# Adding the residual of a decoder block's second FFN layer: accumulating transfers in place of loads and GpSimd additions

## The chip, the cores and the metric

The kernel runs on one core of a Trainium2 chip. The metric is the device time of one execution in microseconds (us), the median of several runs. The engines are TensorE (PE in the profile, with PEld for its weight loads), VectorE (DVE), ScalarE (ACT), GpSimd (POOL) and SyncE (SP, which issues transfers). Each engine works through its own list of instructions in order; semaphores tie the lists together.

## What is computed

One block of a decoder: a token mixer with a residual, then an FFN with a residual, then a final norm. The change touches the FFN's second product and its residual.

```python
def reference(x, ...):
    ...
        h = h + jnp.einsum('bse,ed->bsd', mixed, w_out)
        hn2 = rmsnorm(h, norm2_g)
        up = jnp.einsum('bsd,df->bsf', hn2, w_up)
        act = jnp.square(jax.nn.relu(up))
        h = h + jnp.einsum('bsf,fd->bsd', act, w_down)
    return rmsnorm(h, final_g)
```

There are 2048 tokens, a model width of 1024 and an FFN width of 4096, all in float32.

## The kernel before

Tokens are split into four tiles of 512 (`T`), features into chunks of 128 (`P`), so that a chunk of one tile is 128 partitions x 512 columns. The residual `h` lies in DRAM as `hs[j]`, eight such chunks (256 KB each) for each token tile `j`.

Every matrix product is made of float32r parts: an operand is split into a high and a low part (`split`, L143: ACT copies the high part, DVE subtracts to get the low one), and three matmuls, high x high, high x low and low x high, make one product.

The FFN's second layer is the function `down` (L1068). It works on the tokens in two pairs of tiles, `PAIRS` = (0, 1) and (3, 2), called q = 0 and q = 1 below, and uses a fast scheme of seven block products, P1 to P7, in the order P1, P6, P7, P4, P5, P2, P3. P4 and P2 are split once more in the same manner and run for q = 1 and q = 0 together as 28 steps of 12 matmuls (`inner_step`, L1221, matmuls at L1230); the others run straight (matmuls at L1392) as eight steps. For each step, `make` or `make_inner` loads a weight block (tile `wr` or `wq`) and blocks of activations (`ar`), and splits them into `wd` and `ad` (L146 on ACT, L147 on DVE). Two or three steps are made ahead of their use; five buffers of `ad` and three of `wd` exist.

A product that is finished is taken out of PSUM by `evac` (L1199), for each q and each of four chunks n. After P1, ACT copies PSUM to the value tile `p1` (a sum that later becomes a half of the result). After P7, ACT copies to `u3` and `c21`. After P5, DVE adds PSUM to `u3` and to `u2` (L1201). The value tiles hold four chunks each. Into each chunk of `p1`, `c21`, `u3` and `u2` the residual is added once, by `add_residual` (L1194): 4 chunks x 4 tiles x 2 q = 32 additions, of which 8 follow P1, 8 follow P7 and 16 follow P5. The tile `res` that receives the residual has two buffers (the pool `rsp`, L1487).

Right after P5's last chunk, `final` (L1252) sums squares of the finished results of one token tile: ACT squares a chunk (`sq`, L1249) and DVE adds it to `ss` (L1250), first the four chunks of `c21`, then the four of `u3`. P2 comes after P5 on PE, and the splits of its operands stand between these squares and sums on ACT and DVE. P2 adds its inner products to `p1` on DVE (L1237), and P3 then adds to `u2`. A scheduler decides the order of instructions on each engine, from the order of the program and its own model of durations.

Of the kernel before, what the change touches and what calls it, by code (L numbers as in the profile page):

```python
# [8 lines left out]
F32 = mybir.dt.float32  # L9
# [4 lines left out]
ALU = mybir.AluOpType  # L14

P = 128
S = 2048
D = 1024
T = 512
# [21 lines left out]
DA = 2  # L41
# [5 lines left out]
def hymba_block(ctx: ExitStack, tc: tile.TileContext, xT, gains, w_in, pool_w, w_out, w_up, w_down, out):  # L47
    nc = tc.nc
# [84 lines left out]
    hs = [dram.tile([KD, P, T], F32, name=f"hs{j}") for j in range(NT)]  # L133
# [934 lines left out]
    def down(pools):  # L1068
        t8, s8, rs, rt, pupa, pup, rsp, rlp, tmp_, psb = pools
# [122 lines left out]
            return V[name, q]  # L1192

        def add_residual(t, j, half, n):  # L1194
            r = rsp.tile([P, T], F32, tag="res", name="res")
            nc.sync.dma_start(r, hs[j][4 * half + n])
            nc.gpsimd.tensor_tensor(t, t, r, ALU.add)

        def evac(n_, q, n):  # L1199
            b, (j0, j1) = ps[q, n], PAIRS[q]  # L1200
            add = lambda to, of: nc.vector.tensor_tensor(to[:, n], b, of[:, n], ALU.add)  # L1201
            if n_ in CHAIN:
                nc.scalar.activation(val(CHAIN[n_], q)[:, n], b, AF.Copy)
                if n_ == "P7":
                    nc.scalar.activation(val("c21", q)[:, n], b, AF.Copy)
                    add_residual(val("c21", q)[:, n], j1, 0, n)
                elif n_ == "P1":
                    add_residual(val("p1", q)[:, n], j0, 0, n)
            elif n_ == "P5":
                add(val("u3", q), val("u3", q))  # L1210
                add_residual(val("u3", q)[:, n], j1, 1, n)
                add(val("u2", q), val("u2", q))
                add_residual(val("u2", q)[:, n], j0, 1, n)
                if n == 3:
                    final(j1, [val("c21", q)[:, k] for k in range(4)] + [val("u3", q)[:, k] for k in range(4)])
            else:
                add(val("u2", q), val("u2", q))
                if q == 0 and n == 3:
                    final(j0, [val("p1", q)[:, k] for k in range(4)] + [val("u2", q)[:, k] for k in range(4)])
# [153 lines left out]
        for g, (n_, i, kk, qs_) in enumerate(steps):  # L1373
# [5 lines left out]
            t, left_ = made.pop(g)  # L1379
# [46 lines left out]
    def catch_up(n):  # L1426
        for _ in range(n):
            with ExitStack() as behind:
                for ins in (last_split[0], done[0]):
                    if ins:  # L1430
                        behind.enter_context(tc.issue_after(ins.ins))
                later.pop(0)()
# [42 lines left out]
    def ffn():  # L1475
        catch_up(len(later))
        front_scope.close()
        for _ in layer.pop():
            pass
        left_scope.close()  # L1480
        with ExitStack() as scope:
            spool = lambda name, bufs, **kw: scope.enter_context(tc.tile_pool(name=name, bufs=bufs, reuse_waits="tile", **kw))

            rlp, pupa = spool("rlp", 2), spool("pupa", 2)
            spool("even", 1).tile([P, 2 * P // 4], F32, name="even")
            rs, rt, t8 = spool("rs", 5), spool("rt", 6), spool("t8", DA + 1)
            s8, tmp2, pup, rsp = spool("s8", 2 * DA + 1), spool("tmp2", 2), spool("pup", 6), spool("rsp", 2)  # L1487
            down([t8, s8, rs, rt, pupa, pup, rsp, rlp, tmp2, spool("psb", 1, space=PS)])

    x0_scope = inner.enter_context(ExitStack())  # L1490
# [20 lines left out]
    tail(True)  # L1511
    run()
    ffn()


    count = P * H * (TB * NT - 2)
    got = nc.values_load(zeros[0:1, 0:1], min_val=0, max_val=count)
    with tc.If(got < count):
        wlist.clear(), raws.clear(), grans.clear(), gates.clear(), marks.clear()
        state["gran"], last_split[0], last_mm[0], done[:] = 0, None, None, (None, None)  # L1520
        open_pools(front_scope)
        open_big(left_scope)
        open_att(att_scope)
        for j in range(NT):
            far(j)
        att_scope.close()
        open_last(front_scope, last_scope)
        open_out(out_scope)
        tail(False)
        run()  # L1530
        ffn()
# [44 lines left out]
```

## Time and profile before

| | |
|---|---|
| median of 3 runs | 1933.88 us (1931.08 to 1934.98) |
| profiled execution | 1934.94 us, its span 1933.1 us |
| granted TensorE clock | 0.995 |
| down projection | from 1309 us to the end |
| P1's residual additions | 1396 to 1423 us |
| P7's residual additions | 1570 to 1591 us |
| P5's residual additions | 1733 to 1778 us |
| P2 on PE | 1741.6 to 1823 us |

The page gives the busy time of each engine, the busy share by slices of time, the transfers, the chain of work that ended last, and groups of like instructions with their mean duration and the idle time before them. In a group's row, `x16` is the count, the number after the bar the busy time in us, then the mean in ns, then the engine's idle time just before these instructions and what ended it. In a row of stretches the columns are the length, the busy time and count of PE, PEld, DVE, ACT and POOL (or of fewer, where only one line's instructions are taken), the granted clock, the DMA engines' busy share and the GB/s. In a timeline row they are the start, the time taken, the engine, the line and the instruction. A row of waits reads: who waited, for whom, us in total, times, longest.

### The profile page before, as it was taken

To read this page: it belongs to the slowest core of one execution; us is meant where nothing else is said; L and a number is where in the kernel's file an instruction comes from. 1 tells how busy PE (TensorE), PEld (TensorE's weight loads), DVE (VectorE), ACT (ScalarE), POOL (GpSimd) and SP (SyncE) were. 2 spreads that over 40 slices of the span, in tenths; PEclk is the share of its full clock that TensorE was granted. 3 is DMA by queue.
4 is the path that set the end of the run, shared out by engine and by line. 5 is a ranking of instruction groups with operands and counts; after the bars stand their busy time and mean duration, and the time that the engine had idled before them with its cause. 6 is when DMAs were issued, how large, how long until landed. Compare 5 with 4: busy or idle time off the path is not lost.

```text
span 1933.1 us, 26290 instructions
## 1 busy us (share of the span) xinstructions
PE 1902.3 (98%) x9043; PEld 1586.1 (82%) x9043; DVE 1384.3 (72%) x2026; ACT 991.0 (51%) x1580; POOL 205.8 (11%) x399
## 2 busy tenths in 40 slices
PE   9999999999999999999999999999999999999997
PEld 7888888887888888888888888887888888887887
DVE  6887799668876875767678767676554558649874
ACT  5565566455544455555566555553333255425643
POOL 0211123102111120000000000000010020004120
PEclk9999999999999999999999999999999999999999
DMA  6685786888796864567567566679798869958852
GB/s 225 205 270 180 230 278 207 265 311 268 252 359 252 305 203 167 205 242 232 204 234 245 199 221 224 227 271 387 263 334 287 289 234 334 327 195 267 311 206 90
DMA packets 197359, 483.44 MB, mean 250 GB/s; under 512 B 22496, under 2 KB 42976, under 8 KB 193120
## 3 DMA queue, kind: packets, MB, share of 16 engines
q1 hardware_dynamic: 197072, 481.40, 72.2%
q8 instruction: 73, 1.20, 0.3%
q14 instruction: 70, 0.57, 0.1%
q10 hardware_dynamic: 144, 0.26, 0.0%
HBM read 320.10 MB, written 161.48 MB: 249 GB/s over the span
## 4 chain that ended last, share of the span: by engine, by line
PE 88%; DVE 6%; DMA 4%; issue 1%; ACT 1%; POOL 0%; SPq 0%; DVEq 0%; ACTq 0%
PE pb L1392 21%; PE pY L1052 17%; PE pZ L1052 8%; PE pd L175 7%; PE pd L177 7%; PE pd L176 7%; PE pb L1230 6%; PE pX L1052 4%; PE po L672 2%; PE pta L661 1%; PE pr L228 1%; PE pz L614 1%; PE pz L615 1%; PE pm L202 1%; DMA raw<-in_w_in_dram 1%
## 5 line engine op out<-in xcount | busy, mean ns | idle before, releaser
L1392 PE MATMUL pb<-ad,wd 128*128 128x512 f32 x1872 | 429.6, 391 | 4.8 <-ACT ad L146 4.8
L1392 PEld LDWEIGHTS pb<-ad,wd 128*128 128x128 f32 x1872 | 352.4, 189 | 78.4 <-ACT ad L146 5.2
L1052 PE MATMUL pY<-sa,hw 128*128 128x512 f32 x1536 | 364.2, 389 | 1.8 <-ACT u L987 1.8
L1052 PEld LDWEIGHTS pY<-sa,hw 128*128 128x128 f32 x1536 | 288.2, 188 | 62.3 <-ACT u L987 2.7
L175 PE MATMUL pd<-h,hl 128*128 128x512 f32 x752 | 299.9, 399 | 1.4 <-DVE acc L811 0.7
L177 PE MATMUL pd<-h,hl 128*128 128x512 f32 x752 | 297.0, 395 | 0.0
L176 PE MATMUL pd<-h,hl 128*128 128x512 f32 x752 | 296.7, 395 | 0.0
L146 ACT ACTIVATE ad<-ar 128x1024 fp32r<-128x1024 f32 x136 | 142.4, 1052 | 108.1 <-PE pb L1392 66.8
L147 DVE TENSOR_TENSOR ad<-ar,ad 128x1024 fp32r<-128x1024 f32 x136 | 173.3, 1286 | 34.2 <-ACT ad L146 34.2
L1052 PE MATMUL pZ<-sa,hw 128*128 128x512 f32 x768 | 184.6, 389 | 0.0
L1052 PEld LDWEIGHTS pZ<-sa,hw 128*128 128x128 f32 x768 | 144.1, 188 | 29.9
L175 PEld LDWEIGHTS pd<-h,hl 128*128 128x128 f32 x752 | 142.2, 189 | 29.3 <-issue 1.1
L177 PEld LDWEIGHTS pd<-h,hl 128*128 128x128 f32 x752 | 141.8, 189 | 28.0
L176 PEld LDWEIGHTS pd<-h,hl 128*128 128x128 f32 x752 | 142.0, 189 | 27.0
L146 ACT ACTIVATE hl<-raw 128x512 fp32r<-128x512 f32 x168 | 103.9, 630 | 106.7 <-PE pd L177 67.1
L1230 PE MATMUL pb<-ad,wd 128*128 128x512 f32 x672 | 154.1, 390 | 3.8 <-DVE ad L147 3.8
L1230 PEld LDWEIGHTS pb<-ad,wd 128*128 128x128 f32 x672 | 125.6, 188 | 32.0 <-DVE ad L147 6.1
L147 DVE TENSOR_TENSOR hl<-raw,hl 128x512 fp32r<-128x512 f32 x168 | 114.4, 687 | 51.2 <-ACT hl L146 48.0
L146 ACT ACTIVATE wd<-wr 128x1024 fp32r<-128x1024 f32 x48 | 50.9, 1062 | 152.1 <-PE pb L1392 138.5
L147 DVE TENSOR_TENSOR hw<-rt,hw 128x512 fp32r<-128x512 f32 x128 | 87.6, 688 | 56.6 <-ACT hw L146 55.8
L147 DVE TENSOR_TENSOR wd<-wr,wd 128x1024 fp32r<-128x1024 f32 x48 | 58.6, 1222 | 60.2 <-ACT wd L146 60.0
L1052 PE MATMUL pX<-sa,hw 128*128 128x512 f32 x384 | 93.1, 389 | 0.0
(213 smaller groups left out, 2626.0 us busy)
## 6 DMA issues: line engine op xcount, KB each, us to landing
ar<-sd SPq DMA_DIRECT2D x104, 512.0 KB, 5.7
rb<-in_w_up_dram SPq DMA_DIRECT2D x32, 1024.0 KB, 6.0
wr<-in_w_down_dram SPq DMA_DIRECT2D x64, 512.0 KB, 5.5
sd<-a SPq DMA_DIRECT2D x112, 256.0 KB, 3.5
raw<-in_w_in_dram SPq DMA_DIRECT2D x50, 512.0 KB, 4.6
sd<-s SPq DMA_DIRECT2D x96, 256.0 KB, 3.5
raw<-in_w_out_dram SPq DMA_DIRECT2D x32, 512.0 KB, 6.0
ar<-sdi SPq DMA_DIRECT2D x32, 512.0 KB, 5.6
```

The lines of the kernel that those rows point to most:

```text
L146: nc.scalar.activation(hi, src, AF.Copy)
L147: return nc.vector.tensor_tensor(lo, src, hi.bitcast(F32), ALU.subtract)
L175: nc.tensor.matmul(ps, hl[:, 0, c], hi, start=(k == 0), stop=False)
L176: nc.tensor.matmul(ps, hl[:, 0, c], lo, start=False, stop=False)
L177: mm = nc.tensor.matmul(ps, hl[:, 1, c], hi, start=False, stop=(k == n - 1))
L202: marks["pm"] = nc.tensor.matmul(pm[:, c:c + 1], ss[:, c * P:(c + 1) * P], inv[n], start=(i == 0), stop=(i == len(parts) - 1))
L228: mm = nc.tensor.matmul(pr[:, b * P:(b + 1) * P], yr[:, x, b:b + 1].to_broadcast([P, P]), identr, start=(b == 0 and x == 0), stop=(b == TB ...
L614: nc.tensor.matmul(pz, qa[:, qsl], k, start=first, stop=False, skip_group_check=not (first and last))
L672: nc.tensor.matmul(po[:, p * 256 + to:p * 256 + to + hi - lo], vw[:, 2 * p + v], at[:, x, lo:hi], start=(p == 0 and n == 0 and x == 0), sk ...
L1052: nc.tensor.matmul(t, w[:, wx, c], a[:, ax, c % 2], start=first and c == 0 and x == 0, stop=last and c == G - 1 and x == 2, skip_group_che ...
L1230: nc.tensor.matmul(b, t[:, wx, 2 * (kk % 2) + c, i * P:(i + 1) * P], a[:, ax, c], start=p in ("P1", "P5", "P2") and kk == 0 and c == 0 and ...
L1392: nc.tensor.matmul(ps[q, n], t[:, wx, c, n * P:(n + 1) * P], left_[q][:, ax, c], start=(n_ in ("P1", "P5", "P3") and kk == 0 and c == 0 an ...
```

## The change

`add_residual` loads nothing into a tile of its own any more. GpSimd issues one transfer for each chunk that reads the residual from DRAM and adds it onto the value tile in SBUF (`accum_op=ALU.add`). The pool `rsp` with its two tiles goes. As before, each of the 32 chunks has its own instruction, on the same engine and behind the same DVE or ACT instruction.

```diff
         def add_residual(t, j, half, n):
-            r = rsp.tile([P, T], F32, tag="res", name="res")
-            nc.sync.dma_start(r, hs[j][4 * half + n])
-            nc.gpsimd.tensor_tensor(t, t, r, ALU.add)
+            nc.gpsimd.dma_start(t, hs[j][4 * half + n], accum_op=ALU.add)
...
-            s8, tmp2, pup, rsp = spool("s8", 2 * DA + 1), spool("tmp2", 2), spool("pup", 6), spool("rsp", 2)
+            s8, tmp2, pup, rsp = spool("s8", 2 * DA + 1), spool("tmp2", 2), spool("pup", 6), None
```

The lines behind `add_residual` move up by two: L1201 becomes L1199, L1249 and L1250 become L1247 and L1248. PE's list is the same in both. The lists of DVE, ACT and SP differ in a few places.

DVE at the end of P5, before: `u3` and `u2` are the value tiles, `pb` the PSUM bank, `ss` the sum of squares, and the two splits of `ad` and `wd` are for P2.

```order
L1201 TENSOR_TENSOR u2_14505<-pb_15773,u2_14505 128x512
L1250 TENSOR_TENSOR ss_16297<-ss_16297,sq_16308 128x512
L1201 TENSOR_TENSOR u3_15079<-pb_15780,u3_15079 128x512
L1201 TENSOR_TENSOR u2_14505<-pb_15780,u2_14505 128x512
L147 TENSOR_TENSOR ad_16236<-ar_16234,ad_16236 128x1024
L1201 TENSOR_TENSOR u3_15125<-pb_15787,u3_15125 128x512
L1201 TENSOR_TENSOR u2_14534<-pb_15787,u2_14534 128x512
L1201 TENSOR_TENSOR u3_15125<-pb_15794,u3_15125 128x512
L1201 TENSOR_TENSOR u2_14534<-pb_15794,u2_14534 128x512
L1250 TENSOR_TENSOR ss_16297<-ss_16297,sq_16311 128x512
L1201 TENSOR_TENSOR u3_15125<-pb_15801,u3_15125 128x512
```

The same place of the change:

```order
L1199 TENSOR_TENSOR u2_14486<-pb_15738,u2_14486 128x512
L1199 TENSOR_TENSOR u3_15060<-pb_15745,u3_15060 128x512
L1199 TENSOR_TENSOR u2_14486<-pb_15745,u2_14486 128x512
L147 TENSOR_TENSOR ad_16201<-ar_16199,ad_16201 128x1024
L1199 TENSOR_TENSOR u3_15098<-pb_15752,u3_15098 128x512
L1199 TENSOR_TENSOR u2_14515<-pb_15752,u2_14515 128x512
L1248 TENSOR_TENSOR ss_16246<-ss_16246,sq_16257 128x512
L1199 TENSOR_TENSOR u3_15098<-pb_15759,u3_15098 128x512
L1199 TENSOR_TENSOR u2_14515<-pb_15759,u2_14515 128x512
L1199 TENSOR_TENSOR u3_15098<-pb_15766,u3_15098 128x512
L1199 TENSOR_TENSOR u2_14515<-pb_15766,u2_14515 128x512
```

The first sum with a square of `u3` stands five instructions later (behind the next two additions, a split and two more), and the second one moves behind the last addition, to the place just ahead of the weight split for P2's fifth step.

ACT at the same time, before: the squares `sq` of `u3` among the splits for P2.

```order
L146 ACTIVATE ad_16231<-ar_16227 128x1024
L1249 ACTIVATE sq_16308<-u3_15079 128x512
L146 ACTIVATE ad_16236<-ar_16234 128x1024
L1249 ACTIVATE sq_16311<-u3_15079 128x512
L146 ACTIVATE wd_16403<-wq_16401 128x1024
L146 ACTIVATE ad_16408<-ar_16404 128x1024
L1249 ACTIVATE sq_16314<-u3_15079 128x512
```

And of the change:

```order
L146 ACTIVATE ad_16196<-ar_16192 128x1024
L146 ACTIVATE ad_16201<-ar_16199 128x1024
L1247 ACTIVATE sq_16257<-u3_15060 128x512
L1247 ACTIVATE sq_16260<-u3_15060 128x512
L146 ACTIVATE wd_16336<-wq_16334 128x1024
L146 ACTIVATE ad_16341<-ar_16337 128x1024
L1247 ACTIVATE sq_16263<-u3_15060 128x512
```

The first square has moved behind a split; the second is still the last instruction ahead of the weight split.

SP at the same time, as a difference (`res` are the residual loads, `ar` and `wq` the blocks for P2):

```order
 L1141 DMA ar<-sdi_0_3_428 128x1024
-L1196 DMA res<-hs_281 128x512
-L1196 DMA res<-hs_282 128x512
-L1196 DMA res<-hs_281 128x512
 L1141 DMA ar<-sdi_1_0_429 128x1024
-L1196 DMA res<-hs_282 128x512
-L1196 DMA res<-hs_281 128x512
-L1196 DMA res<-hs_283 128x512
-L1196 DMA res<-hs_284 128x512
 L1136 DMA wq<-wi_P_0_461 128x1024
 L1141 DMA ar<-sdi_1_1_430 128x1024
```

The residual loads between P2's loads are gone, and P2's loads keep their order. On POOL, the 32 transfers stand in the places of the 32 additions; each goes by one of eight semaphores, and waits for the transfer eight before it.

## The prediction

> **What bounds the kernel now.** I read the page's first part, then the busy time by stretches, then the waits.
>
> ```profile
> PE 1902.3 (98%) x9043; PEld 1586.1 (82%) x9043; DVE 1384.3 (72%) x2026; ACT 991.0 (51%) x1580; POOL 205.8 (11%) x399
> PE pb L1392 <- ACT ad L146: 4.8, 1, 4.8
> PE pb L1230 <- DVE ad L147: 3.8, 4, 1.3
> PE pY L1052 <- ACT u L987: 0.7, 1, 0.7
> ACT sq L1249 <- POOL u L1197: 8.7, 4, 3.4
> ```
>
> TensorE (PE) has work nearly throughout, so an edit on another engine counts only where it starves PE or feeds it sooner. The waits of the last 600 us leave two places of size: 4.8 us where the down projection begins (at 1310 us, before any residual is added), and 3.8 us in the matmuls of L1230, where PE waits for a split that VectorE (DVE) makes. L1230 runs twice, once as product P4 and once as product P2, with 336 equal matmuls each time. Busy time in these two stretches:
>
> ```profile
> 1578.56:1654.72 76.16, 76.16 (x336) 62.72 (x335) 1.00 0.86 302
> 1741.60:1823.18 81.58, 77.78 (x336) 62.34 (x335) 1.00 0.86 300
> ```
>
> P4 takes 76.16 us, P2 takes 81.58 (the columns are length, PE busy, weight loads busy, clock, DMA share, GB/s). The clock is 1.00 in both. So P2 loses **5.42 us**, a little more than the labelled 3.8. The timeline shows where:
>
> ```profile
> 1752.84 2.63 PEld L1230 LDWEIGHTS pb<-ad,wd 128*128 128x128 f32 x12 [0.17 <-DVE ad L147]
> 1759.05 6.06 PE L1230 MATMUL pb<-ad,wd 128*128 128x512 f32 x25 [0.57 <-DVE ad L147]
> 1766.46 5.51 PE L1230 MATMUL pb<-ad,wd 128*128 128x512 f32 x23 [1.35 <-DVE ad L147]
> 1772.67 5.74 PE L1230 MATMUL pb<-ad,wd 128*128 128x512 f32 x24 [0.71 <-DVE ad L147]
> 1779.59 43.59 PE L1230 MATMUL pb<-ad,wd 128*128 128x512 f32 x191 [1.17 <-DVE ad L147]
> ```
>
> The stalls lie between 1752 and 1779 us, and then 191 matmuls run without one. In the same time GpSimd (POOL) makes 16 of its 32 residual additions. DVE, all forms apart, from 1733 to 1778 (first four rows) and in a stretch without POOL additions (last two):
>
> ```profile
> 1733.00:1778.00 45.00, 42.38 (x183) 33.69 (x182) 45.00 (x44) 22.88 (x28) 27.86 (x16) 1.00 0.76 248
> L147 DVE TENSOR_TENSOR ad<-ar,ad 128x1024 fp32r<-128x1024 f32 x10 | 15.8, 1590 | 0.0
> L147 DVE TENSOR_TENSOR wd<-wq,wd 128x1024 fp32r<-128x1024 f32 x6 | 10.7, 1786 | 4.2 <-ACT wd L146 4.2
> L1250 DVE TENSOR_TENSOR ss<-ss,sq 128x512 f32<-128x512 f32 x8 | 9.6, 1198 | 0.0
> ...
> L147 DVE TENSOR_TENSOR ad<-ar,ad 128x1024 fp32r<-128x1024 f32 x14 | 17.0, 1222 | 1.1 <-ACT ad L146 1.1
> L1250 DVE TENSOR_TENSOR ss<-ss,sq 128x512 f32<-128x512 f32 x3 | 2.1, 689 | 0.1
> ```
>
> DVE is busy for 45.00 of 45 us, but its instructions are longer than elsewhere: a split takes 1590 or 1786 ns in place of 1222, a sum of squares 1198 in place of 689. That is 10 x 0.368 + 6 x 0.564 + 8 x 0.509 = 3.7 + 3.4 + 4.1 = **11.2 us** of DVE time lost while POOL adds. POOL's additions are what differs between the stretches, so I take them for the cause. The Trainium skill, "SBUF — State Buffer", section "Who interferes with whom", says the same of a DVE instruction with two SBUF inputs beside a GpSimd instruction that reads SBUF, and that DMAs do not meet the engines' ports; by that rule all of the 11.2 us would come back.
>
> **The change, part by part.** *The 16 additions of P5.*
>
> ```profile
> L1197 POOL TENSOR_TENSOR u<-u,res 128x512 f32<-128x512 f32 x16 | 27.9, 1752 | 158.6 <-DVE u L1201 144.8 <-DMA res<-hs 13.1 <-DVE ss L1250 0.6
> 1733.15 1.28 DVE L1201 TENSOR_TENSOR u<-pb,u 128x512 f32<-128x512 f32 x2
> 1734.35 1.94 DVE L147 TENSOR_TENSOR ad<-ar,ad 128x1024 fp32r<-128x1024 f32 x1
> 1749.23 1.32 DVE L147 TENSOR_TENSOR wd<-wq,wd 128x1024 fp32r<-128x1024 f32 x1
> 1750.47 2.31 DVE L147 TENSOR_TENSOR ad<-ar,ad 128x1024 fp32r<-128x1024 f32 x1
> ```
>
> They take 27.9 us of POOL and go. What this gives PE is not 11.2 us but at most the 5.42 it loses. P2 has 28 steps of 12 matmuls, 76.16 / 28 = 2.72 us each; the fifth is due at 1741.60 + 4 x 2.72 = 1752.5, and its left operand was ready at 1750.47 + 2.31 = 1752.8: late from here on. I lay the new DVE order out with undisturbed durations (split 1.22, addition of PSUM 0.68, sum 0.69): pair of additions from 1733.15, split to 1735.6, six additions to 1739.7, split to 1740.9, pair to 1742.2, sum to 1742.9, six additions to 1747.0, sum to 1747.7, weight split to 1748.9, left split to **1750.1**. That is 2.4 us ahead of its due time, and the next ones stay ahead (seventh step: 1754.4, due 1757.9; ninth: 1760.8, due 1763.4). So if nothing new is waited for, P2 runs at 76.16 us.
>
> *What is new: the accumulating transfers.* No POOL transfer and no accumulation is in this trace. Nearest rows: the loads that go, all transfers on the same DRAM tensor, and the squares on ScalarE (ACT) that wait.
>
> ```profile
> L1196 SPq DMA_DIRECT2D res<-hs x32: 319/319/999, 1309.7 to 1772.2; - x32
> DMA to landing us min/median/max: 2.6/3.7/7.6
> ...
> DMA to landing us min/median/max: 2.1/4.4/10.5
> ...
> 1736.36 1.06 ACT L146 ACTIVATE ad<-ar 128x1024 fp32r<-128x1024 f32 x1 [0.48 <-PE pb L1392]
> 1739.67 0.63 ACT L1249 ACTIVATE sq<-u 128x512 f32<-128x512 f32 x1 [2.24 <-POOL u L1197]
> 1741.80 1.07 ACT L146 ACTIVATE wd<-wq 128x1024 fp32r<-128x1024 f32 x1 [1.50 <-PE pb L1392]
> 1749.50 0.63 ACT L1249 ACTIVATE sq<-u 128x512 f32<-128x512 f32 x1 [3.36 <-POOL u L1197]
> ```
>
> Issue on POOL: at least the 0.32 us that SP needs, at most the 1.75 us that POOL spent on the addition. Landing: at least 2.6 us, the fastest plain load; at most twice the slowest transfer on this tensor, 21 us, since source and destination both have to be read. I take 1 + 5 = **6 us** from the end of DVE's addition to landed data, nearer to the median load (3.7) than to twice the extreme. The price in a sentence of its own: the Trainium skill, "DMA: Bandwidth & Descriptors", section "Anatomy of one DMA — SWDGE (gpsimd) path", fits 2.0 us plus bytes over 436 GB/s, which for 256 KB is an estimate of 2.6 us, and would make the margin below wider.
>
> What waits for them: on ACT the squares of u3, and behind these the splits of P2; on DVE the sums. The first u3 tile is added by 1733.8, and DVE wants its square at 1742.2; less 0.63 for the square, that allows 7.7 us, and 10.1 with the 2.4 us that DVE is ahead. The second is added at 1736.3 and stands before the weight split of the fifth step on ACT, which must be done by 1747.7: 1747.7 - 1.06 - 0.63 - 1736.3 = 9.7 us, or 12.1. The fourth (added 1739.0) has 14.8 us by the seventh step's due time. With 6 us none of them holds anything. They are also quicker in sequence than before: there only two load buffers existed, so 16 additions ended at 1777 us (the 1749.50 row shows the fourth square waiting 3.36 us for POOL); now eight may be in flight.
>
> *The other 16 transfers.* P1's and P7's lie where PE has no idle time:
>
> ```profile
> 1396.00:1423.00 27.00, 27.00 (x121) 22.36 (x120) 18.12 (x13) 11.21 (x15) 11.43 (x8) 1.00 0.81 284
> 1570.00:1591.00 21.00, 21.00 (x94) 17.40 (x93) 12.73 (x9) 16.36 (x25) 13.09 (x8) 1.00 0.61 192
> ```
>
> Their disappearance gives nothing. Their replacements cost nothing while covered: p1 is read next in P2, over 300 us later; c21 first at the end of P4's fourth step, 1578.56 + 4 x 2.72 = 1589.4, while its first tile is copied at about 1570, a cover of 19 us. In P3, u2 is read again some 100 us on.
>
> *SP.* 32 issues of 0.32 us go, with their waits for a free buffer:
>
> ```profile
> SPq L1196 <- POOL u L1197: 15.5, 13, 2.3
> SPq L1196 <- DMA res<-hs: 10.4, 9, 1.9
> ```
>
> Loads queued behind them leave earlier; PE shows hardly a wait for a load in this half, so I count zero. The bytes from DRAM stay; 32 x 256 KB more are read from SBUF, 8 MB beside 483, with the DMA engines 0.76 busy in P5's stretch: nothing.
>
> **Sum.** 5.4 us less in P2, of which I leave 0.4 for a first step that may still be tight: **-5.0 us**. The profiled execution took 1934.94 (span 1933.1 and 1.84 around it), so 1929.9 for it; it lies 1.06 above the median of the three runs, so 1928.9 against 1933.88, or -0.26%.
>
> **Rivals.** *A, the transfers are late.* The place is ACT's squares of u3 and the splits behind them. Up to 10.1 us of latency nothing happens, then each further us is one of PE; before's own loss of 5.42 is passed at 15.5 us. At the upper bound, 1.75 + 21 = 22.8 us, P2 loses 12.7, and the kernel is 7.3 slower: 1941.2. For it: reading and writing the same tile is a longer task than any in the trace, and 256 KB loads on this tensor took up to 10.5. Against: median 4.4. Chance 0.17.
>
> *B, POOL still disturbs DVE.* If writing 16 transfers costs as much of the ports as 16 additions, DVE's 11.2 us stay lost, and only the earlier squares are won: 0 to 2.7 us, 1933.9 to 1931.2. For it: POOL is at work in the same places. Against: an issue need not read the tile. Chance 0.20.
>
> *C, DVE holds the transfers back.* In 1733 to 1778 DVE is never idle; if POOL could prepare a transfer only in DVE's pauses, DVE would run on to its first sum at 1742.2, wait there for issue, landing and square, 1.75 + 3.7 + 0.63 = 6.1, and lose 6.1 - 2.4 = 3.7 there: 1.7 us faster than before, 1932.2; with a landing of 10.5 it is 5.1 slower, 1939.0. The Trainium skill, "DMA: Bandwidth & Descriptors", section "SWDGE vs HWDGE vs iDMA", has GpSimd write descriptors into SBUF and lets DVE lock it out in two-port modes; no run here shows it yet. Chance 0.08: POOL's additions, which do meet DVE, were stretched but never kept out.
>
> **How the numbers follow.** Forecast 0.55, with its own range of 1928.0 to 1931.0. I call a change of more than 0.2% (3.9 us) faster or slower, which is about what a measurement here can tell from none. The forecast puts 0.53 on faster and 0.02 on the same; B 0.02 faster and 0.17 the same, with 0.01 slower; A 0.03 the same and 0.14 slower; C 0.01 faster, 0.03 same, 0.04 slower. Together: faster 0.56, same 0.25, slower 0.19. The range runs from 1927.0 (all of the 5.42, and a us and a half of scatter) to 1938.0, where A and C have begun but not reached their bounds.
>
> **What would show it.** DVE's splits and sums near 1222 and 689 ns in 1733 to 1778; no idle time of PE before L1230 in P2, which then takes about 76.2 us; transfers landing in 4 to 8 us; the squares of u3 waiting for a DMA, harmlessly. I am wrong if the squares wait until past 1748 us and PE's idle time moves behind them (A, C), or if DVE's durations stay long (B).

## The result and the profile after

Over 22 runs of each on the same chip the change takes 1928.77 us (1925.58 to 1935.04) against 1933.62 (1929.44 to 1936.88). The ratio is 0.9975, with a 95% interval of 0.9969 to 0.9982: 0.25% faster, 4.9 us by the medians. Predicted were 1928.9 and -5.0.

The first view of the profile after is that of P2's 336 matmuls (the change's lines are two lower, so L1228 for L1230): a stretch, and the two rows of PE's timeline around it.

```profile
1739.97:1816.14 76.17, 76.17 (x336) 62.85 (x335) 1.00 1.02 330
...
1724.79 15.35 PE L1390 MATMUL pb<-ad,wd 128*128 128x512 f32 x67
1739.97 76.33 PE L1228 MATMUL pb<-ad,wd 128*128 128x512 f32 x336
```

P2 took 81.58 us before and takes 76.17 now, one unbroken row in place of five with idle time between them. That is 5.41 us, all of what P2 had lost. The spans of the two profiles differ by 5.8 us: 1.6 lie ahead of P2 (it starts at 1739.97 in place of 1741.60) and 5.4 in it, and 1.2 come back behind it. In the kernels below, which share the program up to the residuals, P2's start moved between 1736.25 and 1743.75 from profile to profile. So only the stretch itself is compared from here on, and the medians for the whole.

DVE's instructions from the end of P5, by form, and then the busy times of that stretch:

```profile
L147 DVE TENSOR_TENSOR ad<-ar,ad 128x1024 fp32r<-128x1024 f32 x13 | 15.7, 1222 | 4.5 <-ACT ad L146 4.5
L147 DVE TENSOR_TENSOR wd<-wq,wd 128x1024 fp32r<-128x1024 f32 x7 | 8.6, 1223 | 5.2 <-ACT wd L146 5.2
L1248 DVE TENSOR_TENSOR ss<-ss,sq 128x512 f32<-128x512 f32 x9 | 6.1, 688 | 1.0 <-ACT sq L1247 1.0
...
1731.00:1777.00 46.00, 46.00 (x205) 38.09 (x204) 39.50 (x49) 24.03 (x30) 14.04 (x16) 1.00 1.02 275
```

Splits and sums are at their undisturbed 1222 and 688 ns, and DVE is idle for 6.5 of 46 us where before it had not a single pause. The transfers are another matter. The queues of the same stretch, and the transfers' landing times:

```profile
q0 software_dynamic: 2304, 4.20, 51.2%
q1 hardware_dynamic: 3503, 8.41, 50.2%
...
ar<-sdi SPq DMA_DIRECT2D x12, 512.0 KB, 9.7
u<-hs POOLq DMA_DIRECT2D x16, 256.0 KB, 12.0
wq<-in_w_down_dram SPq DMA_DIRECT2D x6, 256.0 KB, 11.5
```

The 16 accumulating transfers move 4.20 MB and hold half of the DMA engines' time; the two queues together fill the engines (the share of 1.02 in the stretch). The transfers land 12 us after their issue in the median, and P2's own loads take 1.8 and 3.4 times as long as they did (the same stretch of before has 5.4 us for `ar` and 3.4 for this `wq`).

### The profile page after: what moved, and what is told of

Same layout as the page of the kernel before. It is cut to its first block, busy times and chain, and to the rows that moved or that the text cites. A ratio compares the mean times of both kernels' runs of the same rounds, so it can differ in the third digit from the quotient of the medians.

```text
span 1927.3 us, 26270 instructions
## 1 busy us (share of the span) xinstructions
PE 1903.3 (99%) x9043; PEld 1588.9 (82%) x9043; DVE 1365.9 (71%) x2026; ACT 990.4 (51%) x1580; POOL 177.3 (9%) x399
## 4 chain that ended last, share of the span: by engine, by line
PE 92%; DVE 4%; DMA 2%; issue 1%; POOL 1%; ACT 1%; SPq 0%; DVEq 0%; ACTq 0%; POOLq 0%
PE pb L1390 22%; PE pY L1052 17%; PE pZ L1052 9%; PE pb L1228 8%; PE pd L175 8%; PE pd L176 8%; PE pd L177 8%; PE pX L1052 4%; PE po L672 2%; PE pta L661 1%; PE pm L202 1%; PE pz L614 1%; PE pr L228 1%; PE pz L615 1%; PE pb L1333 1%
## 5 line engine op out<-in xcount | busy, mean ns | idle before, releaser
L147 DVE TENSOR_TENSOR ad<-ar,ad 128x1024 fp32r<-128x1024 f32 x136 | 164.8, 1222 | 39.6 <-ACT ad L146 39.5
L1228 PE MATMUL pb<-ad,wd 128*128 128x512 f32 x672 | 152.7, 389 | 0.0
L1228 PEld LDWEIGHTS pb<-ad,wd 128*128 128x128 f32 x672 | 126.1, 188 | 26.2
```

Of the source, the lines that this page charges most:

```text
L147: return nc.vector.tensor_tensor(lo, src, hi.bitcast(F32), ALU.subtract)
L1228: nc.tensor.matmul(b, t[:, wx, 2 * (kk % 2) + c, i * P:(i + 1) * P], a[:, ax, c], start=p in ("P1", "P5", "P2") and kk == 0 and c == 0 and ...
```

## The experiments

All ratios are to the kernel before, run beside them on the same chip. Its median in the table is that beside the change; beside the other kernels it was 1934.15 to 1934.32 us. P2's length is that of its 336 matmuls in the one profile of each kernel, 76.16 us where nothing is lost.

| kernel | median us | ratio (95% interval) | P2, us |
|---|---|---|---|
| before | 1933.62 | 1 | 81.58 |
| the change | 1928.77 | 0.9975 (0.9969 to 0.9982) | 76.17 |
| p5_only | 1929.12 | 0.9979 (0.9970 to 0.9988) | 76.16 |
| p1p7_only | 1934.54 | 1.0000 (0.9990 to 1.0011) | 82.17 |
| p5_resident | 1933.16 | 0.9998 (0.9988 to 1.0007) | 80.49 |
| p5_memset | 1928.42 | 0.9972 (0.9961 to 0.9983) | 76.16 |
| p5_dve_resident | 1932.71 | 0.9992 (0.9980 to 1.0004) | 79.35 |
| no_p5 | 1929.18 | 0.9972 (0.9961 to 0.9983) | 76.16 |
| plain | 1929.56 | 0.9976 (0.9965 to 0.9987) | 76.16 |
| extra4 | 1931.47 | 0.9974 (0.9962 to 0.9987) | 76.97 |
| extra8 | 1928.32 | 0.9958 (0.9941 to 0.9975) | 76.16 |
| late4 | 1935.15 | 1.0003 (0.9994 to 1.0013) | 80.06 |
| late8 | 1938.56 | 1.0019 (1.0010 to 1.0028) | 85.08 |

### Which of the 32 residuals matter: p5_only and p1p7_only

The 16 residuals after P5, and the 16 others, changed alone. In p5_only:

```diff
+        def accum_residual(t, j, half, n):
+            nc.gpsimd.dma_start(t, hs[j][4 * half + n], accum_op=ALU.add)
...
-                add_residual(val("u3", q)[:, n], j1, 1, n)
+                accum_residual(val("u3", q)[:, n], j1, 1, n)
...
-                add_residual(val("u2", q)[:, n], j0, 1, n)
+                accum_residual(val("u2", q)[:, n], j0, 1, n)
```

> Only the 16 residuals after P5 become accumulating transfers; those after P1 and P7 stay loads and POOL additions. Theory (the gain is DVE's time in P5 and P2): the whole gain stays, 4 to 6 us against the kernel before, ratio about 0.9975; P2 takes 76.2 us, and DVE's splits between the end of P5 and 45 us later are near 1222 ns. Rival (the gain comes from all 32, through fewer loads on SP's queue): about half the gain, 2 to 3 us.

p1p7_only has the reverse: `add_residual` accumulates, and P5's two calls go to a function with the old three lines.

> Only the 16 residuals after P1 and P7 become accumulating transfers; those after P5 stay loads and POOL additions. Theory: no gain, within 1 us of the kernel before; P2 still loses 4 to 6 us over 76.2, with PE waiting for splits on DVE. Rival (the gain comes from all 32): 2 to 3 us faster.

Measured: the whole gain is in p5_only, none in p1p7_only, which loses 6.0 us in P2. DVE's forms in the stretch, in p1p7_only:

```profile
L147 DVE TENSOR_TENSOR ad<-ar,ad 128x1024 fp32r<-128x1024 f32 x11 | 19.4, 1766 | 0.0
L1253 DVE TENSOR_TENSOR ss<-ss,sq 128x512 f32<-128x512 f32 x8 | 10.0, 1247 | 0.0
```

Splits of 1766 ns again, where p5_only has 1219. The rival of a gain through SP's queue falls.

### Contention or late additions: p5_resident

Before, two things came together in P5: POOL's additions lengthened DVE's instructions, and with two load buffers the additions themselves were late. This kernel keeps the first and takes the second away.

```diff
+        def resident_residual(t, j, half, n):
+            nc.gpsimd.tensor_tensor(t, t, val("p1", PAIRS.index(next(p for p in PAIRS if j in p)))[:, n], ALU.add)
...
-                add_residual(val("u3", q)[:, n], j1, 1, n)
+                resident_residual(val("u3", q)[:, n], j1, 1, n)
...
-                add_residual(val("u2", q)[:, n], j0, 1, n)
+                resident_residual(val("u2", q)[:, n], j0, 1, n)
```

> As before, but POOL's 16 additions after P5 add a chunk of p1 that lies in SBUF in place of the residual: no loads, no waits for two load buffers (the residual of those 16 chunks is left out and p1 added in its place). Theory (POOL's reads lengthen DVE's instructions): DVE still loses 8 to 12 us in that stretch, splits of 1500 ns and more in the mean, and P2 still loses 3 to 6 us over 76.2; the time is within 2 us of before. Rival (the loss came from the additions being throttled by two load buffers, so that squares came late): P2 takes 76.2 to 77 us and the kernel is 4 to 6 us faster.

DVE's forms and POOL's:

```profile
L147 DVE TENSOR_TENSOR ad<-ar,ad 128x1024 fp32r<-128x1024 f32 x12 | 19.6, 1643 | 0.0
L1204 DVE TENSOR_TENSOR u<-pb,u 128x512 f32<-128x512 f32 x16 | 10.0, 675 | 0.0
L1253 DVE TENSOR_TENSOR ss<-ss,sq 128x512 f32<-128x512 f32 x9 | 9.4, 1041 | 0.0
L147 DVE TENSOR_TENSOR wd<-wq,wd 128x1024 fp32r<-128x1024 f32 x6 | 8.4, 1402 | 4.2 <-ACT wd L146 4.2
...
L1195 POOL TENSOR_TENSOR u<-u,p 128x512 f32<-128x512 f32 x16 | 29.4, 1876 | 143.1 <-DVE u L1204 143.1
```

No load is waited for (POOL's idle time ends with DVE's additions alone), yet DVE still loses 12 x 0.42 + 9 x 0.35 + 6 x 0.18 = 9.3 us, P2 loses 4.3, and the time is that of before. The contention is the larger part of the loss; about 1.1 us of P2's 5.4 are left for the late additions, if the two parts simply add (p1p7_only, which also loads P5's residuals, loses 6.0).

DVE's additions from PSUM, which have one input in SBUF, keep their 675 ns beside the same work of POOL (685 in the change). And the mean of a split mixes two cases. In the traces of before, p1p7_only and p5_resident a split or sum is longer, by up to 1.1 us, only where it begins while one of POOL's additions is under way. Where DVE begins first, its instruction keeps its 1.2 or 0.7 us, and it is POOL's addition that takes up to 2.4 us in place of 1.3.

### Reading or any work: p5_memset

As p5_resident, but the new function is one line:

```diff
+        def write_residual(t, j, half, n):
+            nc.gpsimd.memset(t, 0.0)
```

> As before, but POOL's 16 additions after P5 are memsets of the same chunks: POOL writes and reads nothing (the residual and the value of these chunks are left out). Theory (it is POOL's reading that meets DVE's second input): DVE's splits and sums stay at 1222 and 689 ns, P2 takes 76.2 us, 4 to 6 us faster than before. Rival (any POOL work on SBUF lengthens DVE's instructions): splits of 1400 ns and more in the mean, and P2 loses 2 us or more.

DVE's splits and POOL's memsets:

```profile
L147 DVE TENSOR_TENSOR ad<-ar,ad 128x1024 fp32r<-128x1024 f32 x15 | 18.1, 1214 | 0.0
...
L1195 POOL MEMSET u<- 128x512 f32 x16 | 8.4, 527 | 148.7 <-DVE u L1204 147.9
```

POOL writes the same chunks and DVE doesn't notice. A memset is shorter than an addition (527 ns against 1876) and meets fewer instructions, but five of the 16 begin inside a split or a sum, and all 16 take 0.53 us, where p5_resident's additions in such a place take 1.7 to 2.4. So it is POOL's reading that meets those instructions of DVE which have both inputs in SBUF. The other order is hardly tried here: no split or sum begins more than 0.1 us before the end of a memset. The Trainium skill, "SBUF — State Buffer", section "Who interferes with whom", has it so: a GpSimd instruction that only writes doesn't contend with them. The trace agrees, with 1214 and 1643 ns.

### DVE's time as the price: p5_dve_resident

As p5_resident, with `nc.vector.tensor_tensor` in place of `nc.gpsimd.tensor_tensor`.

> As p5_resident, but DVE makes the 16 additions of p1 in place of POOL (the residual of these chunks is left out and p1 added in its place). No POOL work in the stretch, but 16 x 0.69 = 11.0 us more of DVE's own, about what POOL's additions took from it before (11.2 us). Theory (DVE's time between P5 and P2 is what PE pays for): P2 loses 3 to 6 us over 76.2, with splits of 1222 ns, and the time is within 2 us of the kernel before. Rival (something else about POOL's additions, such as the squares waiting for them, makes the loss): P2 at 76.2 to 77.5 us and the kernel 3 to 6 us faster than before.

P2 loses 3.2 us, with splits at 1218 ns, and the time is 1.4 us under before's by the medians (1934.15 beside it), with an interval that includes no change. An addition on DVE of its own costs PE somewhat less than POOL's interference did (3.2 against 4.3 in p5_resident, both with a resident operand), but it is the same currency: some 10 us of DVE in this stretch are 3 to 5 us of PE.

### Whether anything is left: no_p5

As the change, with `pass` for P5's residuals.

> As the change, but the 16 residuals after P5 are left out altogether, transfers too. Theory (with accumulating transfers P2 loses nothing more): same time as the change within 1 us, 4 to 6 us faster than before; the loads of ar and wq in that stretch land in about 5 and 3.5 us in place of 10 and 11. Rival (the transfers still cost PE something outside the labelled waits): 1 to 3 us faster than the change.

P2 at 76.16 us, and a ratio that can't be told from the change's. `ar` lands in 4.8 us and `wq` in 3.3. So in the change the transfers' weight on the DMA engines costs P2 nothing, and no other way of adding the residual can win more in P2.

### What makes the transfers heavy: plain

```diff
-            nc.gpsimd.dma_start(t, hs[j][4 * half + n], accum_op=ALU.add)
+            nc.gpsimd.dma_start(t, hs[j][4 * half + n])
```

> As the change, but POOL's 32 transfers overwrite the value tile with the residual in place of adding to it (the product's part of those chunks is left out). Same queue, same waits. Theory (the accumulation itself is what makes these transfers heavy: 16 of them took 51% of the DMA engines' time for 4.2 MB, 5.6 us per MB, against 2.8 for the other queue): software queue at 25 to 30% in the same stretch, landing in 4 to 6 us in place of 12; time as the change within 1 us, since P2 loses nothing either way. Rival (the POOL queue is slow whatever the transfer does): still about 50% and 10 us or more.

The queue of POOL in 46 us of P5 and P2, then POOL's issues and their landing:

```profile
q0 software_dynamic: 1270, 4.15, 24.0%
...
L1195 POOL DMA_DIRECT2D u<-hs x16 | 8.6, 538 | 158.4 <-DVE u L1199 156.7 <-issue 0.7 <-DMA u<-hs 0.6
...
u<-hs POOLq DMA_DIRECT2D x14, 256.0 KB, 6.3
```

The same bytes take 24.0% in place of 51.2%, 46 x 0.240 / 4.15 = 2.7 us of all engines per MB against 5.6, and land in 6.3 us in place of 12.0, a little over the 4 to 6 expected. With the accumulation the engines' time and the landing are twice as long on the same queue, so the queue is not to blame.

### How late is too late: extra4 and extra8, then late4 and late8

Behind the first `u3` chunk, 4 or 8 more accumulating transfers:

```diff
+                if q == 0 and n == 0:
+                    for e in range(4):
+                        add_residual(val("p1", e // 4)[:, e % 4], PAIRS[e // 4][0], 0, e % 4)
```

> As the change, with 4 more accumulating transfers on POOL behind the first u3 chunk (they add the residual once more to four chunks of p1). Theory (up to about 12 us from DVE's addition to landed data nothing is lost, then a us of PE for each us): the second u3 chunk landed 9.4 us after its addition in the change; 4 more at 1.5 us of all DMA engines each make it 15, so P2 loses about 3 us and the kernel is 2 to 4 us slower than the change. Rival (late residuals are covered anyway, by ACT's and DVE's slack): within 1 us of the change.

> As extra4, with 8 more transfers. Theory: the second u3 chunk lands about 21 us after its addition, 9 us past the margin: P2 loses 7 to 11 us and the kernel is slower than the one before the change, by 2 to 6 us. Rival: as the change, or a loss of less than 3 us.

Neither told anything of late residuals. The program's order didn't bind the scheduler, and POOL issued the extra transfers right after P1's (the last one at 1431.9 us in extra8), 300 us too early. extra4's 0.8 us in P2 begin at the fourteenth step: the block `ar` for its left operand landed 13.9 us after its issue, and the operand was ready 0.3 us after its due time (1743.75 + 13 x 2.72 = 1779.1). In late4 and late8 the order is fixed:

```diff
-                add_residual(val("u3", q)[:, n], j1, 1, n)
+                if q == 0 and n == 0:
+                    last = add_residual(val("u3", q)[:, n], j1, 1, n)
+                    for e in range(4):
+                        with tc.issue_after(last.ins):
+                            last = add_residual(val("p1", e // 4)[:, e % 4], PAIRS[e // 4][0], 0, e % 4)
+                    marks["extra"] = last
+                else:
+                    with tc.issue_after(marks["extra"].ins):
+                        add_residual(val("u3", q)[:, n], j1, 1, n)
```

> As extra4, but the 4 more accumulating transfers are held between the first u3 chunk's transfer and the second's by the order of issue, which extra4's were not (they add the residual once more to four chunks of p1). Theory (up to about 12 us from DVE's addition to landed data nothing is lost, then a us of PE for each us): the second u3 chunk, 9.4 us in the change, is at about 15 with four transfers of 1.5 us of all DMA engines ahead, so P2 loses about 3 us and the kernel is 2 to 4 us slower than the change. Rival (late residuals are covered by ACT's and DVE's slack): within 1 us of the change.

> As late4 with 8 more transfers. Theory: the second u3 chunk lands about 21 us after its addition, 9 us past the margin: P2 loses 7 to 11 us and the kernel is 7 to 11 us slower than the change, 2 to 6 us slower than the kernel before. Rival: a loss of less than 3 us, so still faster than before.

In late4, ACT's second and third squares of `u3`, and PE where it stands still behind them and again 20 us later:

```profile
1749.59 0.63 ACT L1255 ACTIVATE sq<-u 128x512 f32<-128x512 f32 x1 [4.80 <-DMA u<-hs]
1754.07 0.63 ACT L1255 ACTIVATE sq<-u 128x512 f32<-128x512 f32 x1 [3.85 <-DMA u<-hs]
...
1758.10 19.47 PE L1236 MATMUL pb<-ad,wd 128*128 128x512 f32 x83 [0.59 <-DVE ad L147]
1778.70 0.50 PE L1236 MATMUL pb<-ad,wd 128*128 128x512 f32 x1 [1.13 <-ACT ad L146]
```

In late8, the second square, and PE at the same two places:

```profile
1761.17 0.63 ACT L1255 ACTIVATE sq<-u 128x512 f32<-128x512 f32 x1 [12.05 <-DMA u<-hs]
...
1762.80 0.54 PE L1236 MATMUL pb<-ad,wd 128*128 128x512 f32 x1 [2.13 <-ACT ad L146]
1784.01 0.73 PE L1236 MATMUL pb<-ad,wd 128*128 128x512 f32 x2 [0.83 <-ACT ad L146]
```

DVE finishes the second chunk's addition 5.4 us ahead of P2's start (1734.5 and 1739.97 in the change, where six additions begin at 1733.86 and take 3.67 together). So it landed about 14 us after it in late4 (P2 starts at 1740.80) and 25 in late8 (1741.46), against 10 in the change (the expectations took 9.4). P2 loses 3.9 and 8.9 us. late4 is level with the kernel before, so some 5 us slower than the change by the ratios, where 2 to 4 were expected; late8 is 0.19% slower than before (0.10 to 0.28). P2's loss in late8 lies in the expected range, but not by the expected mechanism alone.

P2's matmuls begin every 76.16 / 336 = 0.227 us where nothing is lost, and what goes beyond that can be added up by place. Behind the late squares and the splits that follow them late4 loses 1.2 us and late8 3.3. From the fourteenth step on they lose 2.5 and 2.7 to late loads of P2's own: the block `ar` of that step, which was late in extra4 too, landed 13.5 and 13.6 us after its issue. The other 2.9 us of late8 fall in a time of lower clock (last section).

Nor is the margin of 12 us tested. The scheduler, which sees the extra transfers, put the splits of the fifth and sixth step ahead of the second square (in late8 those of the seventh, too), so late4's first idle time hangs on the third square. Late residuals do starve PE, then, as rival A of the prediction has it, but from what lateness on in the change's own order is open.

## Why the prediction was right

**What bounds and where.** P2's 5.4 us, and nothing else, was there to be had, and it came whole: p5_only has all of the gain, p1p7_only none, no_p5 no more.

**DVE's 11.2 us as the cause.** Shown: POOL reading without loads keeps the loss (p5_resident), POOL writing doesn't cause it (p5_memset), and DVE's own work in its place brings most of it back (p5_dve_resident). The rule of the Trainium skill that the prediction leaned on ("SBUF — State Buffer", section "Who interferes with whom") held: without POOL's reads the splits and sums are back at 1222 and 688 ns.

**The layout of DVE's new order.** DVE's timeline after, from P5's end to the fifth step's split:

```profile
1740.20 0.69 DVE L1248 TENSOR_TENSOR ss<-ss,sq 128x512 f32<-128x512 f32 x1 [0.33 <-ACT sq L1247]
1740.81 3.67 DVE L1199 TENSOR_TENSOR u<-pb,u 128x512 f32<-128x512 f32 x6
1745.16 0.69 DVE L1248 TENSOR_TENSOR ss<-ss,sq 128x512 f32<-128x512 f32 x1 [0.68 <-ACT sq L1247]
1746.11 1.23 DVE L147 TENSOR_TENSOR wd<-wq,wd 128x1024 fp32r<-128x1024 f32 x1 [0.26 <-ACT wd L146]
1747.26 1.22 DVE L147 TENSOR_TENSOR ad<-ar,ad 128x1024 fp32r<-128x1024 f32 x1
```

The fifth step's left operand is ready at 1748.48 and due at 1739.97 + 10.88 = 1750.85: 2.4 us ahead, as laid out, although DVE waits 1.3 us on the way. That the two agree to a tenth is luck: the waits were not in the working, and they are made good by DVE's instructions overlapping a little (six additions take 3.67 us, where the working had 4.1).

**The transfers' latency was mis-sized.** Of the six us taken, five were for the landing; it was 12.0 in the median over the 16 (4.3 to 16.9 over all 32). The issue on POOL, 0.87 us in the median, was near the 1 us taken. ACT's rows show what saved the forecast:

```profile
1739.53 0.63 ACT L1247 ACTIVATE sq<-u 128x512 f32<-128x512 f32 x1 [3.73 <-DMA u<-hs]
1744.50 0.64 ACT L1247 ACTIVATE sq<-u 128x512 f32<-128x512 f32 x1 [4.33 <-DMA u<-hs]
1747.65 0.63 ACT L1247 ACTIVATE sq<-u 128x512 f32<-128x512 f32 x1 [0.62 <-DMA u<-hs]
```

The first chunk landed 7.3 us after its addition (1739.5 against 1732.2; allowed 7.7, or 10.1 with DVE's lead), the second 10.0 (allowed 9.7, or 12.1). Over the 16 transfers the landing grows from 6.9 us for the first to 12.7 for the seventh and to 16.9; ACT waits only for the first four chunks of `u3`. The fourth of them landed 13.2 us after its addition, where 14.8 were allowed. That this was enough is in part luck: the second chunk took more than its 9.7 us and needed DVE's lead, and the fourth had 1.6 us left. The estimate of 2.6 us by the Trainium skill's fit ("DMA: Bandwidth & Descriptors", section "Anatomy of one DMA — SWDGE (gpsimd) path") was further off than the prediction's own; the plain transfers of `plain`, beside P2's loads, took 6.3.

**"8 MB beside 483: nothing" was wrong as a step.** The stretch's DMA share went from 0.76 to 1.02, since an accumulating transfer holds the engines twice as long as a plain one, and P2's loads came late. It nearly showed on PE:

```profile
1772.52 1.06 ACT L146 ACTIVATE ad<-ar 128x1024 fp32r<-128x1024 f32 x1 [3.88 <-DMA ar<-sdi]
...
1773.61 1.23 DVE L147 TENSOR_TENSOR ad<-ar,ad 128x1024 fp32r<-128x1024 f32 x1 [2.67 <-ACT ad L146]
```

This is the operand of P2's fourteenth step, due at 1739.97 + 13 x 2.72 = 1775.3 and ready at 1774.8. Its block took 12.3 us to land; in extra4 it took 13.9, and P2 lost 0.8 us. That this step of the prediction cost nothing is luck, by half a us.

**The rivals.** B fell with the splits at 1222 ns. C fell too: DVE worked without a pause from 1731.53 to 1739.87 us, and in that time POOL issued seven transfers and the first of them landed (at 1739.5). A's mechanism exists, as late4 and late8 show. Its break-even of 15.5 us was worked out with the first chunk's 10.1; with the second's 12.1 the same sum gives 17.5, and no kernel here tests either. The nearer danger was one that no rival named, the late loads of P2.

## What to carry to other kernels

Look at whether an instruction's mean duration differs between stretches: a VectorE that is "busy" may be waiting inside its instructions for GpSimd, and the remedy is to take GpSimd's reads out of that stretch, not to speed anything up. An accumulating transfer does this, but cost about twice a plain one here in DMA time and landing; count that against the loads around it, and allow its first readers what it measured here, 7 to 13 us. Of the 32 edits only the 16 counted that lie where the bound engine was being starved.

## What was not expected of the hardware

An accumulating transfer from DRAM onto SBUF took 5.6 us of all 16 DMA engines per MB, a plain one on the same queue 2.7, and its issue kept GpSimd 0.87 us against 0.54 in the median. In late8, P2's matmuls also ran at a granted clock of 0.96 over the stretch, where every other kernel's P2 shows 1.00. The trace has a clock of 0.5 from 1763.1 to 1769.9 us, right behind the idle 2.13 us, and matmuls every 0.43 us there in place of 0.227. The kernel before shows the same fall, 0.50 from 1312.9 to 1319.7, during and behind its wait of 4.8 us for the down projection; p5_resident, idle for 2.08 and 1.13 us in P2, shows none. That idle time brings the fall, and how much of it, is not shown by these single profiles.

```profile
1741.46:1826.54 85.08, 80.48 (x336) 64.38 (x335) 0.96 1.05 320
```
